# The token sums' additions on VectorE instead of GpSimd, and their steps spread over six tiles

## The chip, the cores and the metric

The kernel runs on one core of one Trainium2 chip. The metric is the device time of one execution in microseconds (us); the median of several runs is compared. One core has TensorE (PE, the matrix unit), VectorE (DVE), ScalarE (ACT), GpSimd (POOL) and SyncE (SP, which only starts transfers here). Each works through its own queue of instructions in order; semaphores hold an instruction until what it needs is there.

## The reference

A trunk of two decoder layers over 512 tokens of width 1024, in fp32. Layer 0 mixes tokens by dilated sliding-window attention, layer 1 by a gated linear recurrence; behind each mixer comes a gated feed-forward block with a short causal convolution along the tokens, and RMS norms stand before and behind each part. What matters here is the feed-forward block (`h` is 512 x 1024, the hidden width is 3072):

```
def conv_ffn(x, w_up, conv_w, conv_b, w_down):
    u = causal_dwconv(x @ w_up, conv_w, conv_b)      # three taps
    g, v = u[..., :D_FF], u[..., D_FF:]
    return (jax.nn.gelu(g, approximate=True) * v) @ w_down

for layer in range(2):
    ...
    h = rms_norm(x, norm_ffn_pre[layer])
    h = conv_ffn(h, ffn_w_up[layer], ...)
    x = x + rms_norm(h, norm_ffn_post[layer])
```

## The kernel before

Each fp32 matrix product is done as three products of parts: an operand is split into `hi` (its rounded part, a copy on ScalarE, L153) and `lo` (the rest, a subtraction on VectorE, L154), and `mm3` (L340) adds hi x hi, lo x hi and hi x lo in one PSUM bank. The activations `hT` (a pair of hi and lo, 1024 features by 512 tokens) are the moving operand, and weights arrive by DMA as `raw`, are split by `pump` some tiles ahead of their use and wait as `whi` and `wlo`.

`ffn` goes through w_up in 12 chunks `j` of 256 gate columns and 256 value columns, that is four tiles of 128 columns per chunk. A tile is 24 matmuls of 512 columns (8 slices of features, three passes). Behind each tile, `conv` makes the causal convolution: ScalarE scales the bank into `u` (L679), VectorE adds two shifted taps (L683, two instructions); gate tiles then get a gelu on ScalarE (L695), value tiles are multiplied into their gate on VectorE (L697).

From chunk 3 to chunk 10 the gate tiles are made by `seven`: both gate tiles of a chunk, taken as a 2 x 2 block product, are computed with seven block products instead of eight (Strassen's scheme in a variant with few additions). For this the kernel needs sums of weight blocks (made in place by L205 and L209 on VectorE and accumulating DMAs, L191, on GpSimd's queue), and sums of token blocks, made once per layer by the generator `token_sums`. In `seven` a step's products (L830) go to one of two banks; the copies L836, L840 and L841 on ScalarE and the subtractions L845 and L848 on VectorE move partial results between the banks. Step 5, the first, uses the first token sum; steps 6, 7 and 4 use the others at slots 9, 14 and 20.

`token_sums` runs as a side job: `tick` is called behind each tile, lets every side job do its next step (up to its next `yield`), and then splits the next weights. In each layer it is started with chunk 1, so that its steps fall behind the four tiles of chunk 1 and the three of chunk 2 that come before `seven`. Before the change its steps were:

1. A DMA saves the residual stream to DRAM (`x_kept`, L736), because the sums will lie in its buffer.
2. `both` adds hi and lo of eight quarter blocks of `hT` (L749), all eight on GpSimd: `B` for b11, b12, b22 and b21, two halves each, 128 x 512 elements.
3. b11 less b12 (L766), then split into hi and lo.
4. b12 less b22 (L770), b22 plus b11 (L771), the latter split.
5. b21 less b22 (L775), and b12 split.
6. b21 split.

The order of each engine's queue is the order in which the program issues instructions; nothing reorders them.

Of the kernel before, what the change touches and what calls it, by code (L numbers as in the profile page):

```python
# [11 lines left out]
F32 = mybir.dt.float32  # L12
# [3 lines left out]
ALU = mybir.AluOpType  # L16
# [62 lines left out]
def kernel(  # L79
# [25 lines left out]
    nc = tc.nc  # L105
# [12 lines left out]
    def nm(s):  # L118
        uid[0] += 1
        return f"{s}{uid[0]}"  # L120

    def gen(dt=F32, s="g"):
        return gp.tile([P, 512], dt, tag="g", name=nm(s))
# [28 lines left out]
    def split(hi, lo, raw):  # L152
        nc.scalar.activation(hi, raw, AF.Copy)  # L153
        nc.vector.tensor_tensor(lo, raw, hi.bitcast(F32), op=ALU.subtract)  # L154
# [519 lines left out]
    def ffn(layer, hT, post, pre):  # L674
# [31 lines left out]
        for j in range(SEVEN[0]):  # L706
            if j == 1:
                side(token_sums(hT, T))
            if j < SEVEN[0] - 1:
                feat_tiles(2, hT, lambda b, ps: sink(b, ps, j), j == 0)  # L710
            else:
                feat_tiles(1, hT, lambda b, ps: sink(b, ps, j))
                i = chunk()
                feat_tile(i, 0, hT, lambda ps: sink(2, ps, j))
# [17 lines left out]
    def token_sums(hT, T):  # L732

        assert len(sides) == 1
        d = dp.tile([P, 4, D], F32, name=nm("x_kept"))
        nc.gpsimd.dma_start(d, X[0])  # L736
        kept.append(d)
        homes = cp.tile([P, 4, D], F32R, tag="x_sb", name=nm("T"))
        homes = [homes[:, n] for n in range(4)]
        homes += [cp.tile([P, D], F32R, tag="gain", name=nm("T"), bufs=2) for _ in range(2)]  # L740
        homes = [[h[:, 0:512], h[:, 512:1024]] for h in homes]
        homes += [[gen(F32R, "T") for _ in range(2)] for _ in range(2)]
        homes = [[h.rearrange("p (k t) -> p k t", k=2) for h in hs] for hs in homes]
        yield 1

        def both(k0, n):
            o = gen(s="B").rearrange("p (k t) -> p k t", k=2)
            hi, lo = (h[:, k0 : k0 + 2, n * 256 : n * 256 + 256] for h in hT)
            nc.gpsimd.tensor_tensor(o, hi.bitcast(F32), lo.bitcast(F32), op=ALU.add)  # L749
            return o  # L750

        tt = nc.vector.tensor_tensor
        at = ((0, 0), 0), ((0, 1), 0), ((1, 1), 4), ((1, 0), 4)
        B = {}
        for n, k0 in at:
            for k in range(2):
                B[k, n] = both(k0 + 2 * k, n[1])
        yield 1
        b11, b12, b22, b21 = ([B[k, n] for k in range(2)] for n, _ in at)

        def parted(n, b):
            for k in range(2):
                split(homes[2 * n][k], homes[2 * n + 1][k], b[k])

        for k in range(2):
            tt(b11[k], b11[k], b12[k], op=ALU.subtract)  # L766
        parted(0, b11)
        yield 1
        for k in range(2):
            tt(b12[k], b12[k], b22[k], op=ALU.subtract)  # L770
            tt(b22[k], b22[k], b11[k], op=ALU.add)  # L771
        parted(1, b22)
        yield 1
        for k in range(2):
            tt(b21[k], b21[k], b22[k], op=ALU.subtract)  # L775
        parted(2, b12)
        yield 1
        parted(3, b21)
        T.extend([homes[2 * n], homes[2 * n + 1]] for n in range(4))

# [649 lines left out]
```

## Time and profile before

| | |
|---|---|
| median of three runs | 1470.32 us (1470.17 to 1470.71) |
| the profiled execution | 1470.55 us, span 1468.7 us |
| TensorE busy | 1438.2 us (98%) |
| VectorE busy | 983.2 us (67%) |
| ScalarE busy | 735.2 us (50%) |
| GpSimd busy | 197.6 us (13%) |
| mean granted TensorE clock | 0.991 |

The span is the time from the first to the last instruction in the profile; the execution's own time is some 2 us more. Busy shares are averages over stages with different limits. In rows of instructions, L12 is line 12 of the kernel, `out<-in` names the tiles written and read, `xN` is the number of instructions that were merged into the row, and brackets hold the engine's idle time before the row and what ended it. A row's length runs from the start of its first instruction to the end of its last one, and instructions of an engine overlap a little, so that a row of two is shorter than twice one.

### The profile page before, as it was taken

The numbers are of one execution on the slowest core, as the hardware profiler recorded it, in microseconds if no ns is written. First come the engines' busy times: TensorE is split into PE (matmuls) and PEld (weight loads), VectorE is DVE, ScalarE is ACT, GpSimd is POOL, SyncE is SP. The second block draws the span as 40 slices with busy tenths as digits, with TensorE's granted clock in tenths as the row PEclk, the third lists the DMA queues.
The fourth block names the chain that finished last, engine by engine and source line by source line (L and its number), as shares of the span: only waits on it lengthen the run. The fifth ranks groups of instructions, "written<-read, shape, count | busy, mean of one in ns | idle before, by whom it ended". The sixth has DMA issues, their size and how long they took to land.

```text
span 1468.7 us, 20562 instructions
## 1 busy us (share of the span) xinstructions
PE 1438.2 (98%) x7437; PEld 1233.6 (84%) x7437; DVE 983.2 (67%) x2099; ACT 735.2 (50%) x1644; POOL 197.6 (13%) x327
## 2 busy tenths in 40 slices
PE   9999999999999997999999999999997999999998
PEld 7888888888888885999988888888896899888886
DVE  6767647474745979777774348779788777764333
ACT  7655635353524635555543335588445555553331
POOL 0340514040402131101000001000130111000000
PEclk9999999999999998999999999999998999999999
DMA  7653637272816244554452322433333655453201
GB/s 222 207 147 111 177 101 220 89 231 78 242 66 208 87 158 100 140 126 110 143 201 89 112 72 87 132 112 104 98 122 74 165 121 140 127 187 111 90 0 58
DMA packets 142846, 189.66 MB, mean 129 GB/s; under 512 B 9312, under 2 KB 119352, under 8 KB 142232
## 3 DMA queue, kind: packets, MB, share of 16 engines
q1 hardware_dynamic: 114280, 145.48, 31.0%
q0 software_dynamic: 27616, 41.82, 11.9%
q8 instruction: 58, 0.95, 0.3%
q10 hardware_dynamic: 848, 1.05, 0.2%
q14 instruction: 44, 0.36, 0.1%
HBM read 168.83 MB, written 19.49 MB: 128 GB/s over the span
## 4 chain that ended last, share of the span: by engine, by line
PE 83%; DVE 10%; ACT 5%; issue 1%; DMA 0%; DVEq 0%; ACTq 0%
PE ps L340 36%; PE acc L340 24%; PE ps L830 10%; PE v L1024 7%; DVE wlo L154 4%; DVE u L683 2%; PE v L954 2%; DVE xb L1233 1%; ACT whi L153 1%; PE O L1175 1%; PE S L1120 1%; PE S L1074 1%; ACT sig L1254 1%; PE O L340 1%; PE tr L422 1%
## 5 line engine op out<-in xcount | busy, mean ns | idle before, releaser
L340 PE MATMUL ps<-hT,whi 128*128 128x512 f32 (+1 forms) x2240 | 646.7, 374 | 0.0
L340 PEld LDWEIGHTS ps<-hT,whi 128*128 128x128 f32 x2240 | 405.0, 189 | 68.9
L154 DVE TENSOR_TENSOR wlo<-raw,whi 128x512 fp32r<-128x512 f32 x408 | 291.1, 741 | 191.3 <-ACT whi L153 191.3
L340 PE MATMUL ps<-hT,wlo 128*128 128x512 f32 (+1 forms) x1120 | 416.4, 372 | 0.0
L153 ACT ACTIVATE whi<-raw 128x512 fp32r<-128x512 f32 x408 | 244.4, 626 | 227.1 <-PE acc L340 118.2
L340 PEld LDWEIGHTS ps<-hT,wlo 128*128 128x128 f32 x1120 | 211.6, 189 | 37.3
L340 PE MATMUL acc<-whi,ahi 128*128 128x512 f32 x512 | 199.6, 390 | 0.0
L340 PE MATMUL acc<-whi,alo 128*128 128x512 f32 x512 | 199.3, 389 | 0.1
L340 PE MATMUL acc<-wlo,ahi 128*128 128x512 f32 x512 | 199.2, 389 | 0.0
L147 ACT ACTIVATE whi<-raw,first_w 128x128 fp32r<-128x128 f32 (+1 forms) x432 | 147.0, 426 | 53.3 <-PE ps L340 31.1
L683 DVE SCALAR_TENSOR_TENSOR u<-ps,cols,u 128x511 f32<-128x511 f32 x192 | 143.6, 748 | 42.6 <-ACT u L679 39.2
L148 DVE SCALAR_TENSOR_TENSOR wlo<-raw,first_w,whi 128x128 fp32r<-128x128 f32 (+1 forms) x432 | 139.6, 390 | 1.4 <-ACT whi L147 1.3
L340 PEld LDWEIGHTS acc<-whi,alo 128*128 128x128 f32 x512 | 96.1, 188 | 20.3 <-DVE alo L154 0.5
L340 PEld LDWEIGHTS acc<-whi,ahi 128*128 128x128 f32 x512 | 96.1, 188 | 19.9
L340 PEld LDWEIGHTS acc<-wlo,ahi 128*128 128x128 f32 x512 | 96.1, 188 | 19.9
L679 ACT ACTIVATE u<-ps,cols 128x512 f32<-128x512 f32 x96 | 73.7, 768 | 63.0 <-DVE ps L845 39.2
L1024 PE MATMUL v<-whi,hT 128*128 128x512 f32 x320 | 102.3, 393 | 0.0
L830 PE MATMUL ps<-hT,whi 128*128 128x256 f32 x384 | 72.9, 289 | 21.9 <-ACT part L836 20.8
L830 PE MATMUL ps<-T,whi 128*128 128x256 f32 x512 | 92.8, 280 | 0.0
L191 POOL DMA_DIRECT2D raw<-in_ffn_w_up_dram x32 | 41.5, 1471 | 369.5 <-DVE wlo L154 211.8
L383 POOL DMA_DIRECT2D turned<-T x36 | 19.6, 547 | 530.9 <-DVE T L377 526.1
L830 PEld LDWEIGHTS ps<-hT,whi 128*128 128x128 f32 x384 | 63.5, 197 | 25.5 <-ACT part L836 21.2
(196 smaller groups left out, 1643.7 us busy)
## 6 DMA issues: line engine op xcount, KB each, us to landing
raw<-in_ffn_w_up_dram SPq DMA_DIRECT2D x48, 1024.0 KB
raw<-in_attn_w_qkv_dram SPq DMA_DIRECT2D x67, 512.0 KB
raw<-in_ffn_w_down_dram SPq DMA_DIRECT2D x24, 1024.0 KB
raw<-in_ffn_w_up_dram POOLq DMA_DIRECT2D x32, 256.0 KB, 4.7
raw<-in_lru_w_in_dram SPq DMA_DIRECT2D x8, 1024.0 KB
turned<-T POOLq DMA_DIRECT2D x28, 256.0 KB, 2.6
ft<-turned POOLq DMA_DIRECT2D x112, 64.0 KB, 6.2
vrows<-v SPq DMA_DIRECT2D x16, 256.0 KB
```

Source lines behind the costliest of these rows:

```text
L147: nc.scalar.activation(hi[:, k], raw[:, k], AF.Copy, scale=w)
L148: nc.vector.scalar_tensor_tensor(lo[:, k], raw[:, k], w, hi[:, k].bitcast(F32), op0=ALU.mult, op1=ALU.subtract)
L153: nc.scalar.activation(hi, raw, AF.Copy)
L154: nc.vector.tensor_tensor(lo, raw, hi.bitcast(F32), op=ALU.subtract)
L191: nc.gpsimd.dma_start(to, src, accum_op=ALU.add)
L340: mm(dst, l[a], r[b], start=start and n == 0, stop=stop and n == 2)
L383: nc.gpsimd.dma_start(d, T)
L679: nc.scalar.activation(u, ps, AF.Identity, scale=cc[:, j : j + 1], bias=cc[:, 48 + j : 49 + j])
L683: nc.vector.scalar_tensor_tensor(u[:, d:], ps[:, : S - d], wc, u[:, d:], op0=ALU.mult, op1=ALU.add)
L830: mm(y[b][:, 0:256], W[wa][0][:, k, :], right[n](ha, k), start=n in (1, 5) and k == q == 0, stop=k == 3 and q == 2, skip_group_check=True,)
L954: mm(banks[t], hT[a][:, k, t * P : (t + 1) * P], W[b][k % 2][:, 0, :], start=u == n == 0, stop=u == 3 and n == 5,)
L1024: mm(banks[t], hT[a][:, k, t * P : (t + 1) * P], W[b][k % 2][:, 0, :], start=(k, a, b) == (0, 0, 0), stop=(k, a, b) == (KD - 1, 1, 0),)
```

## The change

The eight additions of `both` go to VectorE. The first four (b11 and b12) stay in the second step; the other four (b22 and b21) get a step of their own two tiles later. The later subtractions and splits move back accordingly, so that the generator has seven steps instead of six: b22 and b12 are split in the sixth, b21 is made and split in the seventh, behind the last tile before `seven`.

```diff
         def both(k0, n):
             o = gen(s="B").rearrange("p (k t) -> p k t", k=2)
             hi, lo = (h[:, k0 : k0 + 2, n * 256 : n * 256 + 256] for h in hT)
-            nc.gpsimd.tensor_tensor(o, hi.bitcast(F32), lo.bitcast(F32), op=ALU.add)
+            tt(o, hi.bitcast(F32), lo.bitcast(F32), op=ALU.add)
             return o
 
         tt = nc.vector.tensor_tensor
-        at = ((0, 0), 0), ((0, 1), 0), ((1, 1), 4), ((1, 0), 4)
-        B = {}
-        for n, k0 in at:
-            for k in range(2):
-                B[k, n] = both(k0 + 2 * k, n[1])
-        yield 1
-        b11, b12, b22, b21 = ([B[k, n] for k in range(2)] for n, _ in at)
+
+        def whole(k0, n):
+            return [both(k0 + 2 * k, n) for k in range(2)]
 
         def parted(n, b):
             for k in range(2):
                 split(homes[2 * n][k], homes[2 * n + 1][k], b[k])
 
+        b11, b12 = whole(0, 0), whole(0, 1)
+        yield 1
         for k in range(2):
             tt(b11[k], b11[k], b12[k], op=ALU.subtract)
         parted(0, b11)
         yield 1
+        b22, b21 = whole(4, 1), whole(4, 0)
+        yield 1
         for k in range(2):
             tt(b12[k], b12[k], b22[k], op=ALU.subtract)
             tt(b22[k], b22[k], b11[k], op=ALU.add)
+        yield 1
         parted(1, b22)
+        parted(2, b12)
         yield 1
         for k in range(2):
             tt(b21[k], b21[k], b22[k], op=ALU.subtract)
-        parted(2, b12)
-        yield 1
         parted(3, b21)
         T.extend([homes[2 * n], homes[2 * n + 1]] for n in range(4))
```

## The prediction

> **What bounds the kernel now.** I read the page first, then the list of TensorE's waits, then the timelines of TensorE, VectorE, GpSimd and ScalarE around the longest wait.
>
> ```profile
> span 1468.7 us, 20562 instructions
> ## 1 busy us (share of the span) xinstructions
> PE 1438.2 (98%) x7437; PEld 1233.6 (84%) x7437; DVE 983.2 (67%) x2099; ACT 735.2 (50%) x1644; POOL 197.6 (13%) x327
> ```
>
> TensorE is busy for 1438.2 of 1468.7 us, so a change pays only through the few places where TensorE stands still. Its waits, over the whole run (columns: total us, times, longest us):
>
> ```profile
> PE ps L830 <- ACT part L836: 20.8, 2, 10.5
> PE warm L1349 <- DVE one L1394: 1.5, 1, 1.5
> PE ps L830 <- ACT ps L841: 1.1, 2, 0.6
> ```
>
> Both L830 entries belong to `seven`, once in each FFN layer, right behind the token sums that the change touches. In TensorE's timeline (start, length, and in brackets the idle time before and what ended it) these are:
>
> ```profile
> 579.24 0.80 PE L830 MATMUL ps<-hT,whi 128*128 128x256 f32 x2 [10.28 <-ACT part L836]
> ...
> 586.52 0.50 PE L830 MATMUL ps<-hT,whi 128*128 128x256 f32 x2 [0.55 <-ACT ps L841]
> ...
> 1139.00 0.58 PE L830 MATMUL ps<-hT,whi 128*128 128x256 f32 x1 [10.51 <-ACT part L836]
> ...
> 1146.27 0.39 PE L830 MATMUL ps<-hT,whi 128*128 128x256 f32 x1 [0.54 <-ACT ps L841]
> ```
>
> So TensorE stops at 568.96 (579.24 less 10.28), restarts at 579.24 with step 3 of the first block product, which accumulates in a bank that L836 must have copied out, and waits again for L841 before step 2 at 586.52. The table of stretches shows that it restarts slowly (last columns: granted clock, DMA share, GB/s):
>
> ```profile
> 574.00:579.20 5.20, 0.00 (x0) 0.00 (x0) 3.96 (x7) 5.20 (x11) 0.00 (x0) 0.50 0.16 45
> 579.20:584.30 5.10, 5.06 (x18) 4.58 (x19) 4.37 (x9) 1.20 (x3) 1.04 (x1) 0.50 0.98 328
> ...
> 1139.00:1144.00 5.00, 5.00 (x18) 4.52 (x19) 4.29 (x7) 1.10 (x3) 0.66 (x1) 0.50 1.00 336
> ```
>
> About 5 us of work after each wait run at half the clock. The work between the two waits is 12 matmuls of 256 columns and 12 of 512. The chain of waits has the same kinds at full clock:
>
> ```profile
> 586.52 3.12 PE ps L830 x24
> 589.63 5.47 PE ps L340 x24
> ```
>
> Half of each makes 1.56 + 2.74 = 4.3 us; it took 579.24 to 585.97, 6.7 us. One layer thus loses 586.52 - 568.96 - 4.3 = 13.3 us here, the other 1146.27 - 1128.49 - 4.3 = 13.5 us.
>
> **Why ScalarE is late.** It waits for VectorE's convolutions, and VectorE lost its time 40 us earlier:
>
> ```profile
> 525.60 1.29 DVE L154 TENSOR_TENSOR wlo<-raw,whi 128x512 fp32r<-128x512 f32 x2 [1.28 <-ACT whi L153]
> ...
> 528.98 12.12 DVE L154 TENSOR_TENSOR wlo<-raw,whi 128x512 fp32r<-128x512 f32 x2
> ...
> 1088.51 12.34 DVE L154 TENSOR_TENSOR wlo<-raw,whi 128x512 fp32r<-128x512 f32 x2
> ```
> ```profile
> 529.44 1.10 POOL L736 DMA_DIRECT2D x_kept<-x_sb  x1
> 530.02 10.52 POOL L749 TENSOR_TENSOR B<-hT,hT 128x512 f32<-128x512 f32 x8
> ```
>
> Two subtractions that take 1.29 us elsewhere take 12.12 us while GpSimd does its eight additions (530.02 to 540.54); VectorE goes on at 541.10. The stall is 10.83 us, in the other layer 11.05 us. From there on VectorE has hardly a gap until `seven` begins.
>
> **The change, part by part.** These rows of VectorE and ScalarE carry the sum:
>
> ```profile
> 551.21 0.69 DVE L154 TENSOR_TENSOR wlo<-raw,whi 128x512 fp32r<-128x512 f32 x1 [1.28 <-ACT whi L153]
> ...
> 561.29 0.68 DVE L770 TENSOR_TENSOR B<-B,B 128x512 f32<-128x512 f32 x1
> 562.01 0.69 DVE L771 TENSOR_TENSOR B<-B,B 128x512 f32<-128x512 f32 x1
> ...
> 576.98 1.53 DVE L683 SCALAR_TENSOR_TENSOR u<-ps,cols,u 128x511 f32<-128x511 f32 x2
> 578.54 0.69 DVE L697 TENSOR_TENSOR u<-u,u 128x512 f32<-128x512 f32 x1
> ...
> 581.68 1.28 DVE L154 TENSOR_TENSOR wlo<-raw,whi 128x512 fp32r<-128x512 f32 x2
> 582.89 0.68 DVE L209 TENSOR_TENSOR raw<-raw 128x512 f32<-128x512 f32 x1
> ...
> 1110.97 0.69 DVE L154 TENSOR_TENSOR wlo<-raw,whi 128x512 fp32r<-128x512 f32 x1 [1.28 <-ACT whi L153]
> ```
> ```profile
> 576.74 2.17 ACT L153 ACTIVATE whi<-raw 128x512 fp32r<-128x512 f32 x4
> 578.82 0.36 ACT L836 ACTIVATE part<-ps 128x256 f32<-128x256 f32 x1
> ...
> 583.60 2.19 ACT L153 ACTIVATE whi<-raw 128x512 fp32r<-128x512 f32 x4 [3.90 <-DVE raw L209]
> ...
> 586.09 0.37 ACT L841 ACTIVATE ps<-ps 128x256 f32<-128x256 f32 x1
> ```
>
> The second restart hangs on VectorE by a fixed piece: L209 ends at 583.57, four copies, L840 and L841 follow on ScalarE without a gap, TensorE starts at 586.52, that is 2.95 us behind L209. How far L209 moves is therefore the sum.
>
> 1. Removed: GpSimd's eight additions per layer, and with them the stall: -10.83 and -11.05 us on VectorE. Behind them in GpSimd's queue stand only DMA issues (L191), which wait for VectorE's splits and not for the additions.
> 2. Added: eight VectorE additions per layer, two SBUF inputs of 512 elements in fp32, the shape of L154. The pair at 581.68 is followed at 582.89, so 0.605 us each in a row: 8 x 0.605 = +4.84 us. Their bounds are 0.605 and the 0.72 of a dependent pair (561.29 to 562.01). They depend on no neighbour, so I take the lower one.
> 3. An idle time that goes: at 551.21 VectorE waits 1.28 us because the split behind the second tile's convolution waits for ScalarE's gelu and copy. The first four additions now stand just there (2.42 us of work): -1.28 us in each layer (1110.97 in the other). The second four stand behind the fourth tile, where no wait was.
> 4. Reordered: the splits of b22 and b12 go behind the sixth tile of the stretch, b21's subtraction and split behind the seventh and last. Nothing is added to VectorE before L209 by this, but on ScalarE the two copies of b21 now stand between the last tile's L679 and L836, and wait for VectorE's convolution, product and subtractions. None of the sums is needed at once: the product that starts `seven` uses the first, whose split stays where it was behind the third tile, and the others come at slots 9, 14 and 20.
>
> L209 therefore moves by -10.83 + 4.84 - 1.28 = -7.27 us in one layer, -11.05 + 4.84 - 1.28 = -7.49 us in the other.
>
> L836 moves less. From the last convolution's start to L209's end were 6.59 us (576.98 to 583.57). Two subtractions and two splits join that stretch, 4 x 0.605 and about 0.1 of waiting, so the convolution starts at 583.57 - 7.27 - 6.59 - 2.5 = 567.2. Its product L697 starts 1.56 later, the second subtraction ends 0.6 + 1.3 after that at 570.7, then come one copy (0.6), four copies (2.08) and L836 (0.36): 573.7. TensorE restarts there, 5.5 us earlier and not 7.27, after a wait of some 4.7 us instead of 10.28.
>
> From 573.7 it needs 4.3 us at full clock (578.0) or 6.7 us as slowly as before (580.4); ScalarE is ready at 586.52 - 7.27 = 579.25. So step 2 starts between 579.25 and 580.4. The clock was seen at half after waits of ten us only; for 4.7 us I take the middle of the two work times, 5.5 us, which arrives at 579.2, plus 0.4 us on average for the cases above it. The Trainium skill, page TensorE: Matmul & The Clock Gate, section "What's actually happening", says that one idle window of about 3.4 us drops the clock and about 3.4 us of sustained work restores it. By that rule the restart costs 1.7 us and step 2 comes at 573.7 + 4.3 + 1.7 = 579.7, an estimate from that page; the 5 us at 0.50 above are longer than its window.
>
> Sum: 7.27 + 7.49 - 2 x 0.4 = 14.0 us less. The profiled execution took 1470.55 us (span 1468.7), which leads to 1456.55; it lies 0.23 above the median of 1470.32, so the forecast is **1456.3 us**. Behind step 2 no wait of TensorE is on the list, so nothing takes the gain back there: TensorE and VectorE are earlier by the same amount.
>
> **Rivals.**
>
> *Slower: the stall is not GpSimd's doing.* Another cause fits the time: the 2 MB copy x_kept is issued at 529.44, just before. If it held VectorE, the stall would stay and the additions would come on top: +4.84 - 1.28 = +3.56 us per layer, 1470.3 + 7.1 = **1477.4 us**. The Trainium skill, page Perfetto Trace Analysis, section "Optimizing Scalar/DVE Operations", advises to move work off a saturated VectorE, even to GpSimd, and VectorE is nearly full here; by that rule the change goes the wrong way. The same passage warns that the two share a read port, and with that warning the trace agrees: 12.12 us beside the additions, 1.29 without them. It decides at an addition (stall share included) dearer than (10.83 + 1.28)/8 = 1.5 us. Against it:
>
> ```profile
> 736.43 1.28 DVE L154 TENSOR_TENSOR wlo<-raw,whi 128x512 fp32r<-128x512 f32 x2
> ```
> ```profile
> 736.48 0.57 POOL L730 DMA_DIRECT2D x_sb<-x_kept  x1 [30.20 <-PE ps L830]
> ```
> ```profile
> x_kept<-x_sb POOLq DMA_DIRECT2D x2, 2048.0 KB, 8.7
> x_sb<-x_kept POOLq DMA_DIRECT2D x2, 2048.0 KB, 8.8
> ```
>
> The copy back, as large and as long (8.8 us), leaves the same pair of subtractions at 1.28 us; x_kept lands at about 538.1 (529.44 + 8.7), three us before VectorE goes on, and the stall ends 0.56 us behind the last addition in both layers. Chance 0.05.
>
> *Much faster: TensorE doesn't stop at all.* If L836 came by 568.96, the clock would stay up and both losses go: 13.3 + 13.5 = 26.8, **1443.5 us**. That needs 4.7 us less before L836 than worked out; b21's copies in front of it speak against. Chance 0.03.
>
> *No change to speak of.* The edit does what it says (the eight additions stand on VectorE in the built program), but the second four or the later splits could meet a wait of their own that eats 7 us a layer. I see none: hT is long written, the homes are free from 538.1 on. Chance 0.02.
>
> **The numbers.** The forecast's case holds 0.90. Its low end takes step 2 at ScalarE's time in both layers (14.8 us) and one more idle time of 1.28 us filled: 1470.3 - 16.1 = 1454.2. Its high end takes 0.72 us per addition (0.92 more per layer) and the slow restart in full (1.15 per layer): 1470.3 - 14.76 + 1.84 + 2.3 = 1459.7. The rivals stay outside; the range needs no more than that. A measurement of this kernel can tell some 0.2% (3 us) from no change: faster by more 0.93, within 0.02, slower 0.05.
>
> **What would show it.** Right: no pair of L154 in that stretch above 1.3 us; eight L749 on VectorE per layer of about 0.69 us each, 0.6 apart; TensorE's wait for L836 about 4.7 us a layer and for L841 at most 1.5; L209 before `seven` about 7.3 us earlier. Wrong: a pair that is still held for 10 us, additions of over 1.5 us, a wait for L836 of 10 us or none, or a new wait of TensorE in the seven tiles before.

## The result and the profile after

| | before | after |
|---|---|---|
| median | 1470.47 us (1470.17 to 1470.71, 4 runs) | 1455.97 us (1455.55 to 1457.39, 4 runs) |
| profiled execution | 1470.55 us, span 1468.7 | 1456.06 us, span 1454.3 |
| VectorE busy | 983.2 us | 971.1 us |
| GpSimd busy | 197.6 us | 178.5 us |

The ratio is 0.9903 (95% interval 0.9886 to 0.9920): 14.5 us less, where 14.0 were forecast. VectorE is busy for 12 us less although it does 16 additions more: some 21.9 us of hold, which counted as busy, go (10.83 and 11.05), and 9.7 us of additions come.

TensorE's waits over the whole run:

```profile
PE ps L830 <- ACT part L836: 8.8, 2, 4.4
PE warm L1349 <- DVE one L1394: 1.5, 1, 1.5
PE v L954 <- ACT hT L442: 0.2, 1, 0.2
```

The wait for L836 fell from 20.8 to 8.8 us, that for L841 is gone. The four places of TensorE's timeline that the prediction quoted (the last is step 2 of the other layer):

```profile
573.23 0.50 PE L830 MATMUL ps<-hT,whi 128*128 128x256 f32 x2 [4.42 <-ACT part L836]
...
579.08 0.40 PE L830 MATMUL ps<-hT,whi 128*128 128x256 f32 x2
...
1125.41 0.80 PE L830 MATMUL ps<-hT,whi 128*128 128x256 f32 x2 [4.42 <-ACT part L836]
...
1131.95 0.39 PE L830 MATMUL ps<-hT,whi 128*128 128x256 f32 x2
```

Step 2 starts 7.44 us earlier than before in the first layer (586.52 to 579.08) and 14.32 us earlier in the second (1146.27 to 1131.95): nearly all of the 14.4 us that the span lost arise between the token sums and these two points. VectorE's timeline of the first layer:

```profile
528.83 1.29 DVE L154 TENSOR_TENSOR wlo<-raw,whi 128x512 fp32r<-128x512 f32 x2
...
536.22 1.29 DVE L154 TENSOR_TENSOR wlo<-raw,whi 128x512 fp32r<-128x512 f32 x2 [1.28 <-ACT whi L153]
537.43 1.53 DVE L683 SCALAR_TENSOR_TENSOR u<-ps,cols,u 128x511 f32<-128x511 f32 x2
538.88 2.49 DVE L749 TENSOR_TENSOR B<-hT,hT 128x512 f32<-128x512 f32 x4
541.29 0.68 DVE L154 TENSOR_TENSOR wlo<-raw,whi 128x512 fp32r<-128x512 f32 x1
...
551.37 2.49 DVE L749 TENSOR_TENSOR B<-hT,hT 128x512 f32<-128x512 f32 x4
553.77 1.29 DVE L154 TENSOR_TENSOR wlo<-raw,whi 128x512 fp32r<-128x512 f32 x2
...
568.88 1.29 DVE L777 TENSOR_TENSOR B<-B,B 128x512 f32<-128x512 f32 x2
...
575.21 0.69 DVE L209 TENSOR_TENSOR raw<-raw 128x512 f32<-128x512 f32 x1
```

The pair that took 12.12 us takes 1.29. Four additions take 2.41 us from the start of the first to the start of what follows (538.88 to 541.29), and the split behind them no longer waits. ScalarE's timeline shows what stands in front of L836 now:

```profile
569.60 1.23 ACT L153 ACTIVATE T<-B 128x512 fp32r<-128x512 f32 x2 [3.18 <-DVE B L777]
570.74 2.17 ACT L153 ACTIVATE whi<-raw 128x512 fp32r<-128x512 f32 x4
572.82 0.36 ACT L836 ACTIVATE part<-ps 128x256 f32<-128x256 f32 x1
```

The two copies of b21 wait 3.18 us for L777, and the four copies and L836 queue behind them.

### The profile page after: what moved, and what is told of

Its sections match the earlier page's. It is cut to its first block, busy times and chain, and to the rows that moved or that the text cites. A ratio compares the mean times of both kernels' runs of the same rounds, so it can differ in the third digit from the quotient of the medians.

```text
span 1454.3 us, 20563 instructions
## 1 busy us (share of the span) xinstructions
PE 1436.9 (99%) x7437; PEld 1233.1 (85%) x7437; DVE 971.1 (67%) x2115; ACT 736.3 (51%) x1644; POOL 178.5 (12%) x311
## 4 chain that ended last, share of the span: by engine, by line
PE 85%; DVE 8%; ACT 5%; issue 1%; DVEq 0%; ACTq 0%
PE ps L340 37%; PE acc L340 24%; PE ps L830 11%; PE v L1024 8%; DVE wlo L154 2%; DVE u L683 2%; PE v L954 2%; DVE xb L1233 1%; ACT whi L153 1%; PE O L1175 1%; PE S L1120 1%; PE S L1074 1%; DVE B L749 1%; ACT sig L1254 1%; PE O L340 1%
## 5 line engine op out<-in xcount | busy, mean ns | idle before, releaser
L340 PEld LDWEIGHTS ps<-hT,whi 128*128 128x128 f32 x2240 | 405.0, 189 | 68.8
L154 DVE TENSOR_TENSOR wlo<-raw,whi 128x512 fp32r<-128x512 f32 x408 | 269.4, 688 | 189.6 <-ACT whi L153 189.6
L683 DVE SCALAR_TENSOR_TENSOR u<-ps,cols,u 128x511 f32<-128x511 f32 x192 | 143.6, 748 | 42.6 <-ACT u L679 39.2
L390 POOL DMA_DIRECT2D ft<-turned x144 | 79.1, 557 | 40.2 <-issue 18.0
L830 PEld LDWEIGHTS ps<-T,whi 128*128 128x128 f32 x512 | 80.1, 189 | 1.6
```

The lines of the kernel that those rows point to most:

```text
L340: mm(dst, l[a], r[b], start=start and n == 0, stop=stop and n == 2)
L390: nc.gpsimd.dma_start(t[32 * c : 32 * c + 32].rearrange("j (b x) -> j b x", b=4), d.rearrange("(b j) (c x) -> c j b x", j=32, c=4)[c],)
L683: nc.vector.scalar_tensor_tensor(u[:, d:], ps[:, : S - d], wc, u[:, d:], op0=ALU.mult, op1=ALU.add)
L830: mm(y[b][:, 0:256], W[wa][0][:, k, :], right[n](ha, k), start=n in (1, 5) and k == q == 0, stop=k == 3 and q == 2, skip_group_check=True,)
```

## The experiments

Three theories were to be told apart: that GpSimd's additions hold VectorE and the change gains what their stall costs less what they cost on VectorE (the forecast); that the 2 MB copy x_kept holds it; and that the even spread of the steps is what gains.

**engine_only: the additions on VectorE, the steps as before.**

```diff
-            nc.gpsimd.tensor_tensor(o, hi.bitcast(F32), lo.bitcast(F32), op=ALU.add)
+            tt(o, hi.bitcast(F32), lo.bitcast(F32), op=ALU.add)
```

> The eight additions on VectorE, but the steps of the token sums as before (all eight in the second step, b21 split behind the sixth tile). Theory (the gain is the stall that goes, the new spread of the steps adds nothing): L209 moves as in the full change, -10.8 + 4.8 - 1.3 = -7.3 us per layer; the copies of b21 do not stand in front of L836, so TensorE waits about 3 us for L836 and up to 3 us for L841; 1455.5 us, within 1.5 us of the full change. Rival (the even spread is worth something by itself): at least 3 us slower than the full change, 1459 us or more.

Measured: 1455.27 us, ratio 0.9901 (0.9886 to 0.9916). TensorE's waits:

```profile
PE ps L830 <- ACT part L836: 5.8, 2, 2.9
...
PE ps L830 <- ACT ps L841: 1.3, 1, 1.3
```

This edit alone has the whole gain; the full change, at 0.9903, adds nothing to it. The copies of b21 cost 1.5 us of waiting, 2.9 us here against 4.4 us in the full change, where the prediction had 1.8; but TensorE then meets the same later point, step 2, at 578.81 instead of 579.08 in the first layer.

**order_only: the new spread, the additions on GpSimd.**

```diff
-            tt(o, hi.bitcast(F32), lo.bitcast(F32), op=ALU.add)
+            nc.gpsimd.tensor_tensor(o, hi.bitcast(F32), lo.bitcast(F32), op=ALU.add)
```

> The new spread of the steps, the additions left on GpSimd. Theory: VectorE is held for as long in sum, in two pieces of about 5.3 us, and b21's copies stand in front of L836 (1.8 us later); the second four additions also queue on GpSimd behind a DMA issue that waits for VectorE. Slower than before by 0 to 5 us: 1470 to 1475 us. Rival (the even spread is what gains): 1463 us or less.

Measured: 1470.38 us (1468.99 to 1471.08), ratio 0.9999 (0.9989 to 1.0009). VectorE and then GpSimd in the first layer:

```profile
528.64 7.10 DVE L154 TENSOR_TENSOR wlo<-raw,whi 128x512 fp32r<-128x512 f32 x2
...
553.76 1.53 DVE L683 SCALAR_TENSOR_TENSOR u<-ps,cols,u 128x511 f32<-128x511 f32 x2
555.32 5.12 DVE L697 TENSOR_TENSOR u<-u,u 128x512 f32<-128x512 f32 x1
```
```profile
529.63 5.55 POOL L749 TENSOR_TENSOR B<-hT,hT 128x512 f32<-128x512 f32 x4
...
554.39 5.49 POOL L749 TENSOR_TENSOR B<-hT,hT 128x512 f32<-128x512 f32 x4
```

The stall splits where the additions split: 5.81 us beside the first four (7.10 less 1.29), 4.43 us beside the second four (5.12 less 0.69). The second four start 25 us behind the issue of x_kept (529.05), which lands in less than 9 us, so x_kept cannot be what holds VectorE there. The spread by itself moved nothing.

**kept_late: x_kept behind the additions.**

```diff
         assert len(sides) == 1
         d = dp.tile([P, 4, D], F32, name=nm("x_kept"))
-        nc.gpsimd.dma_start(d, X[0])
-        kept.append(d)
...
             for k in range(2):
                 B[k, n] = both(k0 + 2 * k, n[1])
+        nc.gpsimd.dma_start(d, X[0])
+        kept.append(d)
         yield 1
```

> The kernel before with the 2 MB copy x_kept issued behind the eight additions instead of ahead of them. Theory (GpSimd's additions hold VectorE): one pair of splits still takes 12 us and ends half a microsecond behind the last addition; no stall while the copy runs behind them; 1470 us within 1.5. Rival (the copy holds VectorE): the stall moves behind the additions, to the 8 to 9 us in which the copy runs.

Measured: 1470.19 us in one run. VectorE, then GpSimd:

```profile
528.59 12.28 DVE L154 TENSOR_TENSOR wlo<-raw,whi 128x512 fp32r<-128x512 f32 x2
540.79 1.52 DVE L683 SCALAR_TENSOR_TENSOR u<-ps,cols,u 128x511 f32<-128x511 f32 x2
542.35 0.69 DVE L697 TENSOR_TENSOR u<-u,u 128x512 f32<-128x512 f32 x1
542.96 1.29 DVE L154 TENSOR_TENSOR wlo<-raw,whi 128x512 fp32r<-128x512 f32 x2
```
```profile
529.18 10.53 POOL L747 TENSOR_TENSOR B<-hT,hT 128x512 f32<-128x512 f32 x8
539.10 1.11 POOL L756 DMA_DIRECT2D x_kept<-x_sb  x1
```

The stall stays with the additions, and the pair at 542.96, beside the copy, takes its ordinary 1.29 us. The full change says the same: it issues x_kept at 529.23, and its pairs at 528.83 and 532.21 take 1.29 and 1.28 us. The rival of the prediction that ended slower has no ground left.

**twice: the full change with every addition made two times.**

```diff
             tt(o, hi.bitcast(F32), lo.bitcast(F32), op=ALU.add)
+            tt(o, hi.bitcast(F32), lo.bitcast(F32), op=ALU.add)
```

> The full change with each of the eight additions made twice, into the same tile. Theory (VectorE sets L836 and L209, and an addition costs 0.60 us there): both come 8 x 0.60 = 4.8 us later in each layer; TensorE waits 9.2 us for L836 instead of 4.4, and step 2 comes 4.5 to 5.9 us later, by how long the clock stays at half: 1465 to 1468 us. Rival (VectorE has room in that stretch, and only the stall counted): 1456 to 1458 us.

Measured: 1467.75 us, ratio 0.9985 (0.9975 to 0.9994), and 10.2 us of waiting for L836 (now one line lower) in each layer:

```profile
PE ps L831 <- ACT part L837: 20.4, 2, 10.2
```

Eight more additions per layer cost 11.8 us in all against the full change, 5.9 per layer; the expected 4.8 were too low because the second of a pair waits for the first. VectorE's rows:

```profile
554.05 0.68 DVE L749 TENSOR_TENSOR B<-hT,hT 128x512 f32<-128x512 f32 x1
554.77 0.69 DVE L750 TENSOR_TENSOR B<-hT,hT 128x512 f32<-128x512 f32 x1
555.38 0.68 DVE L749 TENSOR_TENSOR B<-hT,hT 128x512 f32<-128x512 f32 x1
```

The step from one pair to the next is 1.33 us, 0.72 of it for the dependent one, so four pairs take 5.31 us where four single additions took 2.41: 5.8 us per layer. VectorE has no room in that stretch: what is added there reaches the end at its full price.

**lazy: b12's splits and b21's subtraction and splits moved into the first slots of `seven`.** b21's additions stay where they were.

```diff
         parted(1, b22)
+        T.extend([homes[2 * n], homes[2 * n + 1]] for n in range(4))
+        yield 10
         parted(2, b12)
-        yield 1
+        yield 4
         for k in range(2):
             tt(b21[k], b21[k], b22[k], op=ALU.subtract)
         parted(3, b21)
-        T.extend([homes[2 * n], homes[2 * n + 1]] for n in range(4))
```

> The full change, with the splits of b12 and the subtraction and split of b21 moved into the first slots of seven, where they are needed at slots 14 and 20. Theory: six VectorE instructions (6 x 0.605 = 3.6 us) leave the stretch before L209, and L836 stands right behind the last tile's L679 and four copies: no wait for L836, a wait of about 2 us for L841, clock not at half; step 2 about 3.9 us earlier in one layer and 4.8 in the other: 1447.3 us. Rival (the moved steps come late for steps 7 and 4 or delay the weights of the next chunk): new TensorE waits in the first 20 slots, 1455 us or more.

Measured: 1448.86 us, ratio 0.9857 (0.9843 to 0.9872). The wait for L836 is gone, 2.0 us a layer are left before step 2 (L841 stands in line 842 here):

```profile
PE ps L831 <- ACT ps L842: 4.1, 2, 2.0
```

One point of the expectation failed: the clock. The stretches of the wait and of some work behind it:

```profile
572.80:574.90 2.10, 0.06 (x2) 0.04 (x1) 2.10 (x4) 2.07 (x6) 0.34 (x2) 1.00 0.85 146
575.50:578.90 3.40, 3.40 (x18) 3.40 (x18) 3.15 (x5) 2.18 (x4) 0.42 (x1) 0.50 0.64 79
```

A wait of two us is followed by 3.4 us of busy work at half the clock; the other layer's trace shows the same, from 1125.0 to 1128.4. Half a clock for 3.4 us can cost 1.7 us a layer, and the profiled execution, the longest of the four with 1450.34 us, lies 3.0 us above the expected 1447.3. The other three lie only 1.3 to 1.6 us above it; whether they lost the clock in one layer alone is not shown, because one execution has a trace.

**lazy2: b22's splits and b21's additions too.** Behind b12's subtraction and b22's addition the generator waits eight ticks, splits b22, adds b21 two ticks later, splits b12 another two later and finishes b21 four later (the edit against lazy; the list T is filled ahead of all this):

```diff
+        T.extend([homes[2 * n], homes[2 * n + 1]] for n in range(4))
         yield 1
-        b22, b21 = whole(4, 1), whole(4, 0)
+        b22 = whole(4, 1)
...
             tt(b22[k], b22[k], b11[k], op=ALU.add)
-        yield 1
+        yield 8
         parted(1, b22)
-        T.extend([homes[2 * n], homes[2 * n + 1]] for n in range(4))
-        yield 10
+        yield 2
+        b21 = whole(4, 0)
+        yield 2
         parted(2, b12)
```

> As lazy, and b22's splits and b21's two additions as well are moved into the first slots of seven. Theory: 4 x 0.605 = 2.4 us more leave VectorE before L209, so that ScalarE is ready for step 2 at about 572.5, when TensorE arrives (572.8): no wait at step 2 and no half clock, 2.0 + 1.7 us per layer less than lazy: 1441.5 us. Rival (b22's splits now come too late for step 6 at slot 9): a new wait of 1 to 2 us there, with the clock at half again: 1445 us or more.

Measured: 1447.10 us, ratio 0.9844 (0.9829 to 0.9858): 5.6 us above the theory and in the rival's range, though by another way.

```profile
PE ps L833 <- ACT part L839: 2.1, 2, 1.1
PE warm L1352 <- DVE one L1397: 1.5, 1, 1.5
PE ps L833 <- ACT ps L844: 1.3, 2, 0.6
```

The wait before step 2 fell to 0.6 us and the clock stayed up (mean 0.999). A new wait of 1.1 us a layer came, of the size that the rival said, but elsewhere: not at step 6, but for the next block product's L836 (line 839), behind late copies of b21 on ScalarE, and without a drop of the clock. This wait and the 0.6 us left before step 2 make 3.4 of the 5.6 us over both layers. The rest stays open; the theory also took 1.7 us of half clock a layer off lazy's time, which may not have been paid in both layers there.

**lazy3: as lazy, and of the rest b21's additions alone.** The same as lazy2 with b22's splits left behind the sixth tile (the edit against lazy2):

```diff
-        yield 8
+        yield 1
         parted(1, b22)
-        yield 2
+        yield 9
         b21 = whole(4, 0)
```

> As lazy, and b21's two additions alone moved into the first slots of seven, b22's splits stay behind the sixth tile. Theory: 1.2 us leave VectorE before L209; the wait for L841 shrinks from 2.0 to 0.8 us and the clock may stay up: 1.2 to 2.9 us per layer less than lazy, 1443 to 1446.5 us. Rival (VectorE has room there): as lazy, 1449 us.

Measured: 1445.19 us (1445.12 to 1445.21), ratio 0.9830 (0.9816 to 0.9845), the fastest of all: 10.8 us less than the full change.

```profile
PE ps L833 <- ACT ps L844: 1.6, 2, 0.8
```
```profile
573.70:578.00 4.30, 4.30 (x30) 4.07 (x31) 3.99 (x7) 2.81 (x5) 1.00 (x1) 1.00 0.66 79
```

The wait before step 2 is 0.8 us as expected, and the work behind it runs at full clock. The wait for line 839 that lazy2 had is not there: lazy2 moved two splits more and is 1.9 us slower.

## Why the prediction was right

- *The stall is GpSimd's and goes.* Right. The pair takes 1.29 us; kept_late and order_only show that the stall follows the additions and not x_kept.
- *Eight additions at 0.605 us, 4.84 us.* 2.41 and 2.40 us were measured, 4.81.
- *One idle time of 1.28 us is filled.* Right: the split at 541.29 does not wait, and the other idle times of that kind stayed.
- *L209 moves by 7.27 us.* It ended at 575.90 instead of 583.57, 7.67 us earlier, of which 0.15 had been there since 525.45 (525.60 before). Most of the other 0.25 us is in b22's two splits: before, what followed started 1.39 us behind them (563.95 to 565.34), and now a pair of the four in a row takes 1.21 (563.69 to 566.11).
- *L836 moves less, a wait of 4.7 us is left, b21's copies are the reason.* 4.42 us in both layers, behind the copies that wait for L777; TensorE restarts at 573.23 where 573.7 was worked out. engine_only, without them in front, waits 2.9 us.
- *Step 2 starts 0.4 us behind ScalarE on average, because of the clock.* Right in kind, and the term that differs most between the layers. L841 ends at 578.79 and 1130.97, so step 2 is some 0.2 us behind it in one layer and 0.9 in the other, 0.6 on average. With the same wait of 4.42 us TensorE worked at half the clock for 3.4 us in one layer and 5.0 in the other:

```profile
574.00:577.40 3.40, 3.40 (x13) 3.01 (x13) 2.70 (x6) 1.47 (x3) 1.28 (x1) 0.50 0.90 301
```
```profile
1125.40:1130.40 5.00, 4.99 (x18) 4.50 (x19) 4.27 (x8) 2.77 (x6) 1.28 (x1) 0.50 0.69 216
```

  The way from the restart to step 2 took 5.85 us (573.23 to 579.08) and 6.54 us (1125.41 to 1131.95) instead of 4.3, where the prediction took 5.5. The granted clock shows why the layers differ: in the first it fell at 574.0, 0.8 us behind the restart, and rose at 577.4; in the second it had fallen at 1123.5, 1.9 us ahead of the restart, and rose at 1130.4. That is 3.4 and 6.8 us. The prediction's rule from the Trainium skill (TensorE: Matmul & The Clock Gate, "What's actually happening": a window of about 3.4 us) fits the first layer's 3.4 us; the second layer's 6.8 us are two windows. The same section of the Trainium skill says that the window runs free instead of starting with the work; the different moments of the fall behind the same wait agree with that.
- *The sum.* 7.4 and 6.9 us against the forecast's 6.9 and 7.1; 14.5 against 14.0 on the median. That it is so close is in part luck: the restart was longer than the assumed 5.5 us in both layers, by 0.35 and 1.04 us, while L836 and L209 came 0.3 to 0.5 us earlier in each layer than worked out.

The rule to move work off a full VectorE, the slower rival, failed because VectorE was not full of work: 10.8 of the 44 us between the first tile of chunk 1 (525.1) and TensorE's stop (568.96) were a hold by the engine that the work would move to. The warning in the same passage of the Trainium skill (Perfetto Trace Analysis, "Optimizing Scalar/DVE Operations"), that the two engines share a read port, agrees with the runs: VectorE was held for 10.8 us beside eight additions, for 5.8 and 4.4 us beside four and four, and not without them. That the port is the reason, no run here shows.

## What to carry to other kernels

A row of 12 us among equals of 1.3 us may be a hold and no work, as it was here: look for what another engine does in exactly that time, and count that operation at the price of the hold as well as its own. When such a stall feeds a wait 40 us later, find the one instruction that releases the waiting engine and count only what stands in front of it in its queue; steps that are needed later can be issued behind it, which was worth 10.8 us more here (lazy3), as long as their new place makes no new wait (lazy2). TensorE's short waits cost more than their length as soon as the clock drops.

## What the runs showed of the hardware that was not expected

- The clock drops after much shorter waits than the ten us seen before: 2.04 us (lazy) were followed by 3.4 us at 0.50, while waits of 0.8 us (lazy3) and of 1.1 us (lazy2) left it at full. In these traces the stretches of half clock behind the token sums lasted multiples of some 3.4 us by the granted clock: 10.2 and 13.6 us before (574.0 to 584.2 and 1130.4 to 1144.0), 3.4 and 6.8 after, 3.4 in both layers of lazy. What a wait costs depends on when the clock falls, too, and not on its length alone.
- Not every VectorE instruction seems to be held. In order_only the two L683, which read one operand from PSUM and one tile from SBUF, keep their 1.53 us although GpSimd's second additions begin at 554.39, 0.9 us before they end; the next one, L697 with both inputs in SBUF, is the one that takes 5.12 us. The Trainium skill, page SBUF — State Buffer, section "Who interferes with whom", says that a VectorE instruction with two SBUF inputs contends with a GpSimd instruction that reads SBUF, and one with a single SBUF input does not; the overlap agrees in both layers (5.13 us for L697 in the other), and no run here was made to test it.
